# An RWKV-7 recurrence in chunks: one joined state product, products by turns, and preparation, inverse and finish cut into smaller pieces

## The chip, the cores and the metric

The kernel runs on one core of a Trainium2 chip. A core has a tensor engine (PE, with its weight loads PEld), a vector engine (DVE), a scalar engine (ACT), GpSimd (POOL) and a queue of DMA issues on SyncE (SP). Each works through its own list of instructions in order and waits on semaphores of the others. The metric is the device time of one execution in microseconds.

## The reference

One decoder block over 1024 tokens of width 1024, in float32: an input projection, RWKV-7 time mixing (8 heads of 64), attention over keys that an indexer selects, gates, an output projection and an MLP. The change lies in the time mixing. Per token and head, with a 64 x 64 state S:

```
def step(S, inp):
    r_t, w_t, k_t, v_t, a_t, b_t = inp
    sa = jnp.einsum('bhvk,bhk->bhv', S, a_t)
    S = (S * w_t[:, :, None, :] + sa[..., None] * b_t[:, :, None, :]
         + v_t[..., None] * k_t[:, :, None, :])
    return S, jnp.einsum('bhvk,bhk->bhv', S, r_t)
...
y = ((y - mean) * lax.rsqrt(var + RWKV_GN_EPS) * gn_w + gn_b)
y = (y + bonus) * gate
```

The mean and variance are per head and token; `bonus` is a dot product of r, k and r_k times v.

## The kernel before

The recurrence is computed in 16 chunks of 64 tokens, in 4 groups of 4 chunks. What one group needs is made by two Python generators while the chunks of the group before it run:

- `prep(g, G)` (L871 on), for each of four pairs of heads p: `elem(p)` loads `zt` and `zv`, makes decay products with a scan (`L`) and exponentials (`Pt`), and from them the operands `X` and `B`. Then PE multiplies B by X for each of the two heads and the four chunks (tile `sm<-X,B`), and DVE writes the masked result into `LT` (L938), the transposed B beside it (L946) and `bv` (L953). It yields 17 times.
- `invert(g, G)` (L957 on) inverts the triangular 64 x 64 blocks of `LT`. The 16 x 16 diagonal blocks go to DRAM (`md`) and come back as `Z` with another layout; 28 small DVE operations (L998, L1000) invert them; the result goes to DRAM (`mz`, with a transposed copy `Zt` made on ACT, L1002) and comes back as `R16` and `P16`. Then products `sm<-R,bd`, `sm<-bd,Q`, again `sm<-R,bd` (32 wide) and `sm<-P,bd` fill in the larger blocks, with copies on ACT (L1027, L1032, L1045, L1049) and transposes on DVE (`R<-LT`, L1034) between. It yields 5 times.

`chunk(g, G, c)` (L1053 on) has three steps, each ended by a yield:

1. `A` takes LT times WV for the upper half, then X times the state `cur` (tile `sbd`); ACT copies `rhs` (L1068).
2. `W` is the inverted LT times `rhs`; ACT copies it into `WV` (L1073).
3. `Bp` is the state product over all 128 rows, output in PSUM partitions 0 to 63; eight DVE operations (L1082) write the new state as Bp times decay plus `St`, which POOL made of the old state at the chunk's start (L1059). Then the output products go into partitions 64 to 127 of `A`, and ACT copies `Y` (L1089).

After every second chunk `finish(tt, Yt)` (L1092 on) normalises 128 tokens: scaling by gn_b and gate on DVE (L1103), by gn_w on ACT (L1105), mean and variance, a reciprocal root of ten small DVE operations, four transposes (`sm<-cst,Y`), a product and a sum.

Between these pieces the loop pulls units of a filler: `fill` (gates and one branch projection, 192 units of three products `dn`, 512 columns each) until the last group, `fill2` (branch and output projection, 96 units) in it. Numbers at the top say how many: `FILL`, `FIL3` (filler units behind each of the 12 steps of a group) and `AHEAD` (pieces of the next group's preparation and inverse behind each step); a finish's second piece comes `FIN_LAG` steps later. A scheduler then orders every engine's list when the program is built, keeping the dependences, with the order of the source as priority; `pe()` ties each PE instruction behind the one 32 places before it.

## Time and profile before

| | us |
|---|---|
| median of 3 runs (lowest, highest) | 1817.76 (1809.3, 1817.8) |
| the profiled execution | 1819.81, its span 1818.0 |
| PE busy in the span | 1697.3 |
| DVE busy | 1320.5 |
| ACT busy | 895.2 |
| POOL busy | 833.7 |

In the rows below, L and a number is a line of the kernel; an instruction shows engine, line, operation, tiles written and read, its shape and the number of equal ones. In brackets stands the idle time of the engine ahead of it and what ended that. Records of PE overlap and their ends are modelled, so steps from start to start say more than durations.

### The profile page before, as it was taken

How to read it: one execution, taken by the hardware profiler on the slowest of the kernel's cores; microseconds unless marked ns; L12 is line 12 of the kernel's file. 1: busy time of each engine (PE TensorE's matmuls, PEld its weight loads, DVE VectorE, ACT ScalarE, POOL GpSimd, SP SyncE). 2: the span in 40 equal slices, each digit the busy share in tenths (PEclk: the TensorE clock that was granted, in tenths of full speed). 3: DMA queues.
4: the chain of work that ended last, by engine and by line, in shares of the span. 5: the costliest groups of instructions: out<-in, count | busy, mean ns of one | idle time of the engine just before them, and what ended most of it. 6: DMA issues, size and time to landing. Idle time of an engine off the chain costs nothing.

```text
span 1818.0 us, 27188 instructions
## 1 busy us (share of the span) xinstructions
PE 1697.3 (93%) x9554; PEld 1424.4 (78%) x9554; DVE 1320.5 (73%) x2601; ACT 895.2 (49%) x1751; POOL 833.7 (46%) x761
## 2 busy tenths in 40 slices
PE   6999899849999999989898898999999999999997
PEld 6988887738788777777777797977888888888885
DVE  5689955996777454578666746699988875874988
ACT  5375664717777534245435425463444444444453
POOL 1522566324353334243423532286666656545552
PEclk9999999969999998799878999999999999999999
DMA  5230343212311355336436559415544549653444
GB/s 170 79 116 30 115 141 110 64 41 85 123 35 36 134 138 151 84 109 172 121 88 183 158 159 327 127 53 186 172 147 141 177 145 329 186 162 99 141 148 140
DMA packets 268287, 242.04 MB, mean 133 GB/s; under 512 B 64284, under 2 KB 206934, under 8 KB 268150
## 3 DMA queue, kind: packets, MB, share of 16 engines
q1 hardware_dynamic: 268150, 240.30, 42.3%
q8 instruction: 75, 1.23, 0.3%
q14 instruction: 62, 0.51, 0.1%
HBM read 164.76 MB, written 75.50 MB: 132 GB/s over the span
## 4 chain that ended last, share of the span: by engine, by line
PE 61%; DVE 18%; DMA 6%; POOL 4%; ACT 4%; issue 4%; SPq 1%; POOLq 0%; DVEq 0%; ACTq 0%
PE up L189 24%; PE dn L189 15%; PE sm L189 9%; DVE jk L577 3%; PE sm L192 2%; PE ch L189 2%; PE acc L189 2%; PE dn L243 1%; PE dn L244 1%; DVE w L1328 1%; PE dn L242 1%; DVE Zt L998 1%; PE acc L243 1%; POOL h L1328 1%; PE acc L242 1%
## 5 line engine op out<-in xcount | busy, mean ns | idle before, releaser
L189 PE MATMUL dn<-hT,w 128*128 128x512 f32 (+1 forms) x1488 | 379.5, 402 | 8.3 <-ACT last L673 7.5
L189 PEld LDWEIGHTS dn<-hT,w 128*128 128x128 f32 (+1 forms) x1488 | 274.0, 189 | 67.5 <-ACT last L673 10.1
L189 PE MATMUL up<-h,w 128*128 128x512 f32 x1344 | 312.1, 393 | 6.4 <-DVE w L1328 3.1
L189 PEld LDWEIGHTS up<-h,w 128*128 128x128 f32 x1344 | 252.3, 189 | 63.3 <-DVE w L1328 5.0
L1328 DVE TENSOR_TENSOR w<-st,w 128x512 fp32r<-128x512 f32 x216 | 213.5, 1022 | 75.6 <-ACT w L1327 75.5
L210 POOL TENSOR_TENSOR w<-st,w 128x1024 fp32r<-128x1024 f32 (+2 forms) x75 | 179.7, 2397 | 164.6 <-ACT w L209 139.1
L189 PE MATMUL up<-w 128*128 128x512 f32 x1008 | 246.1, 390 | 2.7 <-DVE w L1328 2.7
L189 PEld LDWEIGHTS up<-w 128*128 128x128 f32 x1008 | 188.6, 188 | 44.5 <-DVE w L1328 5.4
L1327 ACT ACTIVATE w<-st 128x512 fp32r<-128x512 f32 x216 | 127.9, 624 | 158.3 <-PE up L189 49.7
L1621 POOL TENSOR_TENSOR st<-wb,wb 128x512 f32<-128x512 f32 x80 | 120.7, 1512 | 93.9 <-DVE w L1328 73.8
L1483 POOL TENSOR_TENSOR c<-st 128x512 f32<-128x512 f32 x80 | 124.6, 1565 | 52.0 <-DMA st<-in_w_ffn_up 26.2
L209 ACT ACTIVATE w<-st 128x1024 fp32r<-128x1024 f32 (+2 forms) x91 | 94.7, 1041 | 42.0 <-PE acc L244 15.0
L577 DVE TENSOR_SCALAR_CACHE_REDUCE jk<-room,cand 128x384 bf16<-128x384 int16 (+2 forms) x96 | 92.6, 1008 | 15.1 <-ACT jk L590 14.1
L1494 POOL TENSOR_TENSOR C<-C 128x512 f32<-128x512 f32 x64 | 75.5, 1180 | 59.1 <-ACT C L1493 59.1
L243 PE MATMUL dn<-w,hT 128*128 128x256 f32 (+1 forms) x320 | 92.1, 289 | 6.3 <-DVE w L210 6.3
L780 POOL TENSOR_SCALAR sm<-sm,rs 128x128 f32<-128x128 f32 (+7 forms) x64 | 47.8, 748 | 105.1 <-DVE rs L779 55.2
L590 ACT ACTIVATE jk<-room,neg 128x512 bf16<-128x512 int16 (+2 forms) x96 | 78.4, 819 | 33.4 <-POOL neg L598 21.8
L242 PE MATMUL dn<-w,hT 128*128 128x256 f32 (+1 forms) x320 | 92.0, 290 | 0.9 <-ACT hT L272 0.9
L244 PE MATMUL dn<-w,hT 128*128 128x256 f32 (+1 forms) x320 | 92.0, 290 | 0.0
L1328 DVE TENSOR_TENSOR w<-c,w 128x512 fp32r<-128x512 f32 x80 | 82.7, 1046 | 0.4
L189 PE MATMUL sm<-w 128*128 128x512 f32 x288 | 81.1, 389 | 0.0
L1327 ACT ACTIVATE w<-c 128x512 fp32r<-128x512 f32 x80 | 48.8, 627 | 64.4 <-PE up L189 52.0
(336 smaller groups left out, 3546.3 us busy)
## 6 DMA issues: line engine op xcount, KB each, us to landing
st<-hcd SPq DMA_DIRECT2D x112, 256.0 KB
st<-in_w_in SPq DMA_DIRECT2D x54, 512.0 KB
st<-in_w_ffn_up SPq DMA_DIRECT2D x36, 512.0 KB
hcd<-C SPq DMA_DIRECT2D x16, 1024.0 KB
wb<-in_w_ffn_down SPq DMA_DIRECT2D x64, 256.0 KB
hcd<-kc SPq DMA_DIRECT2D x16, 768.0 KB
zd<-ev SPq DMA_DIRECT2D x20, 512.0 KB
gzd<-ev SPq DMA_DIRECT2D x32, 256.0 KB
```

The lines of the kernel that those rows point to most:

```text
L189: pe(nc.tensor.matmul(*args, **kw))
L209: nc.scalar.activation(hi, st[0:rows, 0:n], AF.Copy)
L210: (eng or nc.gpsimd).tensor_tensor(lo, st[0:rows, 0:n], hi.bitcast(F32), op=OP.subtract)
L242: nc.tensor.matmul(ps, l[0], r[0], start=start, stop=False, skip_group_check=shared)
L243: nc.tensor.matmul(ps, l[0], r[1], start=False, stop=False, skip_group_check=shared)
L244: nc.tensor.matmul(ps, l[1], r[0], start=False, stop=stop, skip_group_check=shared)
L577: nc.vector.tensor_scalar(junk, src[b], cand[:, j:j + 1], None, op0=OP.is_ge, op1=OP.add, accum_out=cnt[:, j:j + 1])
L590: nc.scalar.activation(junk, src[b], AF.Sign, bias=neg[:, j:j + 1], accum_out=cnt[:, j:j + 1])
L1327: nc.scalar.activation(hi, src, AF.Copy)
L1328: return eng.tensor_tensor(lo, src, hi.bitcast(F32), op=OP.subtract)
L1483: nc.gpsimd.tensor_tensor(c, src, blocks[LEFT[p][2]], op=OP.add if LEFT[p][1] == "+" else OP.subtract)
L1621: nc.gpsimd.tensor_tensor(c, src, wblocks[RIGHT[p][2], f], op=OP.add if RIGHT[p][1] == "+" else OP.subtract)
```

## The change

- The state is joined into the product: `two` holds two 64 x 64 unit matrices one above the other; a product of `two` and the old state starts `Bp`, and the state products add to it. Two DVE operations then multiply by the decay. `St` and its POOL operation go.
- `in_turn` ties a product behind the one just before it. State and output products alternate, and so do the B,X products of the two heads of a pair.
- `hold` ties the first instruction of a piece of finish, inverse or preparation behind the latest instruction of a chunk's step on the same engine.
- `prep` issues the loads of the next pair a piece earlier and its element-wise work a piece later. `invert` has two more yields, `Zt` and the unit diagonal move to DVE. `finish` has three pieces before the last instead of one, and scales by gn_w on DVE from PSUM.
- The tables: `AHEAD` takes three pieces behind each of the first six steps instead of six behind three; the inverse's chain falls to step 7 and later; `FIL3` has fewer units in the first half. The start has its own table `FIRST`.

```diff
-FILL = [8, 2, 40, 3, 6, 22]
-AHEAD = [6, 6, 6, 0, 0, 0, 0, 0, 1, 1, 0, 10]
-FIN_LAG = 5
+FILL = [0, 0, 0, 0, 5, 7]
+AHEAD = [3, 3, 3, 3, 3, 3, 0, 2, 0, 1, 2, 1]
+FIN = [1, 1, 0, 1]
+FIRST = [3, 6] + [2] * 15 + [2, 9, 4, 14, 3, 3, 3, 2]
-FIL3 = [2, 3, 4, 4, 3, 4, 2, 4, 5, 3, 3, 5]
+FIL3 = [2, 2, 2, 2, 2, 3, 4, 4, 4, 4, 4, 4]
...
+    def in_turn(follows, *args, **kw):
+
+        ins = nc.tensor.matmul(*args, **kw)
+        if follows:
+            after(pe_hist[-1], ins)
+        pe(ins)
...
+            pair = [small(), small()]
+            for c in range(GC):
+                for e in range(2):
+                    r = slice(64 * e, 64 * e + 64)
+                    in_turn(c + e, pair[e][:, c * P:(c + 1) * P], B[r, c, :], X[r, c, p, :], start=True, stop=True)
             for e in range(2):
-                r = slice(64 * e, 64 * e + 64)
                 h = 2 * p + e
-                ps = small()
                 for c in range(GC):
-                    mm(ps[:, c * P:(c + 1) * P], B[r, c, :], X[r, c, p, :], start=True, stop=True)
...
+                if e and p < 3:
+                    ahead = elem(p + 1, *nx)
                 yield
...
+        yield
         for t in range(14, 0, -1):
             r = 15 - t
+            if t == 7:
+                yield
...
-        nc.scalar.activation(Zt[0:64], Z[0:64].rearrange("p s t -> p t s"), AF.Copy)
+        nc.vector.tensor_copy(Zt[0:64], Z[0:64].rearrange("p s t -> p t s"))
...
-                nc.vector.transpose(ce(R32[diag(h)]), LT[0:32, :, h:H:4, 0:32])
+                hold("V", nc.vector.transpose(ce(R32[diag(h)]), LT[0:32, :, h:H:4, 0:32]))
...
+    def hold(eng, ins):
+
+        if eng in own:
+            after(own[eng], ins)
+        return ins
...
-        St = rw.tile([P, 4, P], F32, name="St", tag="St")
-        nc.gpsimd.tensor_tensor(St, cur, G["pc"][:, c, :].unsqueeze(2).to_broadcast([P, 4, P]), op=OP.mult)
...
         Bp = chps()
+        mm(Bp[0:64], two, cur.rearrange("p q n -> p (q n)"), start=True, stop=False, skip_group_check=True)
         for h in range(H):
-            mm(Bp[0:64, h * N:(h + 1) * N], LT[:, h, 2 * C:3 * C], WV[:, h, :], start=True, stop=True)
+
+            in_turn(h, Bp[0:64, h * N:(h + 1) * N], LT[:, h, 2 * C:3 * C], WV[:, h, :], start=False, stop=True,
+                    skip_group_check=True)
+            in_turn(1, A[64:128, h * N:(h + 1) * N], LT[:, h, C:2 * C], WV[:, h, :], start=False, stop=True,
+                    skip_group_check=True)
...
-            for p in range(4):
-                nc.vector.scalar_tensor_tensor(nxt[r, p, r], Bv[0:64, p, e, :], G["pc"][r, c, p:p + 1],
-                                               St[r, p, r], op0=OP.mult, op1=OP.add)
+            own["V"] = nc.vector.tensor_tensor(nxt[r, :, r], Bv[0:64, :, e, :],
+                                    G["pc"][r, c, :].unsqueeze(2).to_broadcast([64, 4, N]), op=OP.mult)
...
-            nc.scalar.activation(o[1][:, cs], o[1][:, cs], AF.Copy, scale=pcol("gnw", p))
...
-        nc.vector.tensor_tensor(o[1], ps, o[1], op=OP.mult)
+        for p in range(4):
+            cs = slice(p * P, (p + 1) * P)
+            nc.vector.scalar_tensor_tensor(o[1][:, cs], ps[:, cs], pcol("gnw", p), o[1][:, cs],
+                                           op0=OP.mult, op1=OP.mult)
...
-                if fin:
-                    f_ = fin.pop(0)
-                    if f_ is not None:
-                        pull(f_, 1)
+                for f_ in fin:
+                    f_[1].pop(0) and pull(f_[0], 1)
+                fin[:] = [f_ for f_ in fin if f_[1]]
                 if g + 1 < NG:
                     n_, m = AHEAD[step], FIL3[step]
-                    for i in range(n_):
-                        pull(nxt, 1)
+                    for i in range(n_ + 1):
                         pull(filler, (i + 1) * m // (n_ + 1) - i * m // (n_ + 1))
-                    pull(filler, m - n_ * m // (n_ + 1))
+                        pull(nxt, i < n_)
```

Three places show how the lists move; a name's number is its buffer. On PE, in group 0, before the change, from the third chunk's last products (`ch<-WV,LT`, 16) to the first product of the inverse and the fourth chunk's start:

```order
L189 MATMUL ch<-WV,LT 64x64 x16
L189 MATMUL dn<-hT_6_85,w 128x512
L189 MATMUL dn<-hT_7_86,w 128x512 x3
L189 MATMUL dn<-hT_0_79,w 128x512 x3
L189 MATMUL dn<-hT_1_80,w 128x512 x3
L189 MATMUL dn<-hT_2_81,w 128x512 x3
L189 MATMUL dn<-hT_3_82,w 128x512 x3
L189 MATMUL sm<-R_7658,bd 128x16 x8
L189 LDWEIGHTS zb
L189 MATMUL ch<-zb 64x2
L189 MATMUL ch<-WV,LT 64x64 x8
L189 MATMUL ch<-sbd_6469,X 128x128 x4
```

With the change, from the fourth chunk's second step; `ch<-sbd,two` and the 16 `ch<-WV,LT` behind it are its third step:

```order
L190 MATMUL ch<-rhs,LT 64x64 x8
L190 MATMUL ch<-sbd_6472,two 64x512
L194 MATMUL ch<-WV,LT 64x64 x6
L190 MATMUL sm<-R_7793,bd 128x16 x8
L190 MATMUL dn<-hT_5_84,w 128x512 x3
L190 MATMUL dn<-hT_6_85,w 128x512 x3
L190 MATMUL dn<-hT_7_86,w 128x512 x3
L190 MATMUL dn<-hT_0_79,w 128x512
L190 MATMUL sm<-bd_7894,Q_7892 16x128 x8
L194 MATMUL ch<-WV,LT 64x64 x10
L190 MATMUL sm<-R_7928,bd 128x32 x8
```

The inverse's first products stood between the third and the fourth chunk, behind 16 filler products and the third chunk's `ch<-WV,LT`; now they stand inside the fourth chunk's third step, and ten of its products come behind them.

On DVE, group 0, before the change, around the third chunk's state update (`sbd_6469`):

```order
L170 SCALAR_TENSOR_TENSOR rq<-rb,rq 128x8
L168 TENSOR_TENSOR rb<-var,rq 128x8
L169 TENSOR_TENSOR rb<-rb,rq 128x8
L170 SCALAR_TENSOR_TENSOR rq<-rb,rq 128x8
L1082 SCALAR_TENSOR_TENSOR sbd_6469<-ch,pc,St 64x64 x8
L983 TENSOR_TENSOR bd_7895<-P_7659,cst 128x1024
L1034 STREAM_TRANSPOSE R_7952<-LT 32x256 x4
L887 SCALAR_TENSOR_TENSOR L<-cst,zt 128x256
L1122 TENSOR_TENSOR fo<-sm,fo 128x512
```

With the change, the middle of the chain `Z` and the third chunk's update (`sbd_6472`), and then the chain's end and the fourth chunk's update (`sbd_6471`):

```order
L1022 TENSOR_TENSOR Z<-Z,Zt 128x10x5
L1020 TENSOR_TENSOR Zt<-Z 128x54
L1112 TENSOR_TENSOR sbd_6472<-ch,pc 64x4x64
L1022 TENSOR_TENSOR Z<-Z,Zt 128x9x6
L1112 TENSOR_TENSOR sbd_6472<-ch,pc 64x4x64
L1152 SCALAR_TENSOR_TENSOR fo<-sm,par,fo 128x128 x2
L1020 TENSOR_TENSOR Zt<-Z 128x56
L1152 SCALAR_TENSOR_TENSOR fo<-sm,par,fo 128x128 x2
L1022 TENSOR_TENSOR Z<-Z,Zt 128x8x7
```

```order
L1020 TENSOR_TENSOR Zt<-Z 128x14
L1022 TENSOR_TENSOR Z<-Z,Zt 128x14
L1024 COPY Zt<-Z 64x256
L1002 TENSOR_TENSOR bd_7894<-P_7794,cst 128x1024
L1056 STREAM_TRANSPOSE R_7928<-LT 32x256 x4
L1112 TENSOR_TENSOR sbd_6471<-ch,pc 64x4x64 x2
L1136 SCALAR_TENSOR_TENSOR fo<-fo,par 128x128 x4
```

The chain straddled the second chunk's update before and lies around the third's now; the transposes `R` stood behind the third chunk's update and now stand between the end of `Z` and the fourth's.

On ACT, group 1, before the change, from the third chunk's `rhs` to its `WV`:

```order
L1068 ACTIVATE rhs<-ch 64x512
L1143 ACTIVATE ev<-dn 128x512
L1105 ACTIVATE fo<-fo,par 128x128 x3
L1112 ACTIVATE ysq<-Y 128x512
L1105 ACTIVATE fo<-fo,par 128x128
L1143 ACTIVATE ev<-dn 128x512
L209 ACTIVATE w<-st 128x1024
L1002 ACTIVATE Zt<-Z 64x256
L1073 ACTIVATE WV<-ch 64x512
```

With the change, the same stretch:

```order
L1094 ACTIVATE rhs<-ch 64x512
L1139 ACTIVATE ysq<-Y 128x512
L460 ACTIVATE ev<-dn 128x512
L217 ACTIVATE w<-st 128x1024
L1174 ACTIVATE ev<-dn 128x512
L1099 ACTIVATE WV<-ch 64x512
```

The scaling `fo` and the copy `Zt` are gone from between the two copies.

## Rows read from the trace of the kernel before

**Rows 1.** The page, part 1: busy time of each engine.
```profile
PE 1697.3 (93%) x9554; PEld 1424.4 (78%) x9554; DVE 1320.5 (73%) x2601; ACT 895.2 (49%) x1751; POOL 833.7 (46%) x761
```
**Rows 2.** Groups: stretch, length, busy per engine (instructions), granted clock, DMA share, GB/s.
```profile
712.95:820.96 108.01, 100.56 (x674) 83.01 (x673) 66.03 (x192) 43.51 (x96) 34.88 (x40) 0.81 0.34 91
820.96:907.73 86.77, 79.74 (x614) 65.44 (x612) 61.38 (x187) 40.51 (x88) 36.50 (x32) 0.94 0.53 148
907.73:997.41 89.68, 80.77 (x568) 65.91 (x569) 57.16 (x182) 37.79 (x80) 29.98 (x28) 0.83 0.48 132
997.41:1069.75 72.34, 64.18 (x548) 56.50 (x547) 41.68 (x89) 28.08 (x42) 34.30 (x22) 0.98 0.51 158
```
**Rows 3.** The same view of two stretches.
```profile
717.50:751.70 34.20, 34.20 (x155) 26.82 (x155) 17.42 (x56) 8.83 (x25) 5.20 (x9) 0.50 0.20 62
...
799.50:871.10 71.60, 66.21 (x526) 54.11 (x524) 58.87 (x174) 38.82 (x85) 28.83 (x30) 1.00 0.60 173
```
**Rows 4.** Timeline of PE: start, duration of the merged records, instruction.
```profile
673.86 0.60 PE L189 MATMUL sm<-f,cst 128*128 128x256 f32 x2
674.10 30.32 PE L189 MATMUL dn<-hT,w 128*128 128x512 f32 x132
...
716.54 2.73 PE L189 MATMUL sm<-P,bd 128*128 128x32 f32 x16 [2.83 <-ACT bd L1045]
...
1048.97 1.90 PE L189 MATMUL ch<-WV,LT 128*64 128x64 f32 x32 [1.74 <-ACT WV L1073]
...
1055.39 1.14 PE L189 MATMUL ch<-WV,LT 64*64 64x64 f32 x16
1056.46 1.16 PE L189 MATMUL ch<-sbd,X 128*128 128x128 f32 x8
```
**Rows 5.** Halves of the groups, DVE alone: length, busy, clock, DMA share, GB/s.
```profile
712.95:778.71 65.76, 36.91 (x117) 0.74 0.29 78
778.71:820.96 42.25, 29.12 (x76) 0.92 0.41 112
820.96:862.71 41.75, 32.88 (x112) 1.00 0.62 173
862.71:907.73 45.02, 28.49 (x76) 0.89 0.44 125
907.73:966.27 58.54, 41.58 (x137) 0.83 0.38 103
966.27:997.41 31.14, 15.58 (x45) 0.84 0.66 186
```
**Rows 6.** Groups of lines, 615 to 1093: busy us, mean ns | idle before, releaser.
```profile
L1105 ACT ACTIVATE fo<-fo,par 128x128 f32<-128x128 f32 x32 | 11.3, 391 | 24.4 <-DVE fo L1103 24.4
...
L1034 DVE STREAM_TRANSPOSE R<-LT 32x256 f32<-32x256 f32 x16 | 7.0, 434 | 30.0 <-ACT LT L1027 29.9
...
L1002 ACT ACTIVATE Zt<-Z 64x256 f32<-64x256 f32 x4 | 2.5, 629 | 10.0 <-DVE Z L1000 10.0
...
L998 DVE TENSOR_TENSOR Zt<-Z 128x14 f32<-128x14 f32 x8 | 1.4, 176 | 25.1 <-DMA Z<-md 25.0
```
**Rows 7.** Timelines of ACT and PE, chunk 2 and the inverse's first product.
```profile
785.17 0.63 ACT L1002 ACTIVATE Zt<-Z 64x256 f32<-64x256 f32 x1 [4.04 <-DVE Z L1000]
785.71 0.57 ACT L1073 ACTIVATE WV<-ch 64x512 f32<-64x512 f32 x1
...
786.33 3.18 PE L189 MATMUL ch<-WV,LT 128*64 128x64 f32 x32 [3.21 <-ACT WV L1073]
...
793.20 1.85 PE L189 MATMUL sm<-R,bd 128*128 128x16 f32 x16
```
**Rows 8.** PE alone in two quarters of a microsecond: length, busy (records), clock.
```profile
1049.70:1049.95 0.25, 0.25 (x12) 1.00 0.00 0
1050.10:1050.35 0.25, 0.25 (x9) 1.00 0.65 205
```
**Rows 9.** Timeline of DVE: a product from PSUM, and a state update.
```profile
675.04 0.41 DVE L953 TENSOR_TENSOR bv<-sm,zv 128x256 f32<-128x256 f32 x1
...
788.42 1.73 DVE L1082 SCALAR_TENSOR_TENSOR sbd<-ch,pc,St 64x64 f32<-64x64 f32 x8 [1.58 <-PE ch L189]
```

More of the change, by code (lines that the diff above doesn't have):

```diff
@@ L858, in c3 @@
         return ap.rearrange("p (c t) -> p c t", c=GC)
+    two = rw.tile([P, C], F32, name="two")
+    for i in range(2):
+        nc.scalar.activation(two[64 * i:64 * i + 64], ident[64 * i:64 * i + 64, 64 * i:64 * i + 64], AF.Copy)
     zb = rw.tile([P, C], BF16, name="zb")
@@ L878, in prep, with loads @@
         nc.gpsimd.memset(scl[64:128], 1.0)
-        def elem(p):
+        def loads(p):
             z = rw.tile([P, 4, GT], F32, name="zt", tag="zt", bufs=1)
@@ L907, in elem @@
             return zv, sq, f, B
-        ahead = elem(0)
+        nx = loads(0)
         yield
+        ahead = elem(0, *nx)
         for p in range(4):
@@ L913, in prep @@
             if p < 3:
-                ahead = elem(p + 1)
+                nx = loads(p + 1)
             ps = small()
@@ L929, in prep @@
             yield
+            pair = [small(), small()]
[3 more added lines that the diff above has]
+                    in_turn(c + e, pair[e][:, c * P:(c + 1) * P], B[r, c, :], X[r, c, p, :], start=True, stop=True)
             for e in range(2):
-                r = slice(64 * e, 64 * e + 64)
                 h = 2 * p + e
-                ps = small()
                 for c in range(GC):
-                    mm(ps[:, c * P:(c + 1) * P], B[r, c, :], X[r, c, p, :], start=True, stop=True)
-                for c in range(GC):
-                    nc.vector.scalar_tensor_tensor(LT[:, c, h, 0:P], ps[:, c * P:(c + 1) * P], scl[:, c, h:h + 1],
-                                                   gmask, op0=OP.mult, op1=OP.mult)
+                    nc.vector.scalar_tensor_tensor(LT[:, c, h, 0:P], pair[e][:, c * P:(c + 1) * P],
+                                                   scl[:, c, h:h + 1], gmask, op0=OP.mult, op1=OP.mult)
+                if e and p < 3:
+                    ahead = elem(p + 1, *nx)
                 yield
@@ L1019, in invert @@
         bd2 = rw.tile([P, 2 * GC, P], F32, name="bd2", tag="zt", bufs=1)
-        spread(nc.vector, bd2, P16, ind8)
+        hold("V", spread(nc.vector, bd2, P16, ind8))
         spread(nc.gpsimd, bd, A32, ind4)
@@ L1050, in invert @@
         yield
-    Ycur = [None]
+    Ycur, own = [None], {}
+    def hold(eng, ins):
+        if eng in own:
+            after(own[eng], ins)
+        return ins
     def chunk(g, G, c):
@@ L1067, in chunk @@
         rhs = rw.tile([64, RW], F32, name="rhs", tag="rhs", bufs=1)
-        nc.scalar.activation(rhs, A[0:64], AF.Copy)
+        own["A"] = nc.scalar.activation(rhs, A[0:64], AF.Copy)
         yield
@@ L1080, in chunk @@
             r = slice(64 * e, 64 * e + 64)
-            for p in range(4):
-                nc.vector.scalar_tensor_tensor(nxt[r, p, r], Bv[0:64, p, e, :], G["pc"][r, c, p:p + 1],
-                                               St[r, p, r], op0=OP.mult, op1=OP.add)
-        for h in range(H):
-            mm(A[64:128, h * N:(h + 1) * N], LT[:, h, C:2 * C], WV[:, h, :], start=False, stop=True,
-               skip_group_check=True)
+            own["V"] = nc.vector.tensor_tensor(nxt[r, :, r], Bv[0:64, :, e, :],
+                                    G["pc"][r, c, :].unsqueeze(2).to_broadcast([64, 4, N]), op=OP.mult)
         if ci % 2 == 0:
             Ycur[0] = rw.tile([P, RW], F32, name="Y", tag="Y", bufs=2)
-        nc.scalar.activation(Ycur[0][64 * (ci % 2):64 * (ci % 2) + 64], A[64:128], AF.Copy)
+        own["A"] = nc.scalar.activation(Ycur[0][64 * (ci % 2):64 * (ci % 2) + 64], A[64:128], AF.Copy)
         yield
@@ L1260, in hybrid_block @@
     pull(first, 1)
-    pull(filler, FILL[0])
-    for _ in range(17):
+    for n_ in FIRST:
+        pull(filler, n_)
         pull(first, 1)
-        pull(filler, FILL[1])
-    pull(filler, FILL[2])
-    pull(first, 99)
     fin = []
@@ L1290, in hybrid_block @@
                 pull(f_, 1)
-                fin += [None] * FIN_LAG + [f_]
+                fin.append((f_, list(FIN)))
         pull(nxt, 99)
-    pull(filler2, FILL[5])
-    for f_ in fin:
-        if f_ is not None:
-            pull(f_, 1)
+    for f_, due in fin:
+        while due:
+            due.pop(0) and pull(f_, 1)
+            pull(filler2, FILL[5])
     pull(filler2, 9999)
```

40 lines of the change are left out of this document (22 added, 18 removed).

## The prediction

> **What bounds the kernel now.** I read the page first, then the stretches, the waits, the timelines of single engines. The page gives TensorE (PE) 93% of the span [rows 1], but its spans overlap, so that share says little. The stretches say more [rows 2]: cut at the first `rhs` copy of each group, the three groups that also prepare the next one last 108.0, 86.8 and 89.7 us (284.5 together); the last, which prepares nothing, 72.3. The work beside them is the same kind, so the difference is what a group pays for preparation and inverse. The granted clock falls there too: 0.81, 0.94 and 0.83 of full, and in one piece of 34 us PE stood at the lower level, 1.2 GHz, throughout, while the neighbouring 72 us had 2.4 GHz [rows 3]. Before that fall PE had sat idle for the inverse (2.8 us before the `P` products), then it ran mostly the small products of preparation [rows 4].
>
> PE's own need is much less. At full clock 16 records of 64 columns take 1.14 us with a tail of 0.2, so 0.93; X times state 0.9; a 512-column filler record 30.32 / 132 = 0.23 [rows 4]. (An f32 product has two records; 32 in a row take 1.90 with tail.) A chunk is 0.93 + 0.9 + 0.93 + 1.86 = 4.6 us, four are 18.4. Preparation takes 16 X,B records for each of four pairs (128 columns like X times state, so 0.11 each and 7.2 a group) and some 6 of other products; the inverse four times 1.8; the filler 3 records a unit, 0.68 us. A group needs some 65 us of the 87 to 108 it gets: PE is not the bound, it waits.
>
> For what? In the first two chunks of a group, for VectorE (DVE): 32.9 of 41.8 us busy in group 1, the one with full clock there [rows 5], the preparation's chain going to and fro between DVE, ScalarE (ACT) and PE. In the last two (chunks 2 and 3, counted from 0 in each group), for queues blocked at the head: DVE stood 30 us before the transposes `R`, 25 us before the first inverse step (a DRAM round trip), ACT 24 us before the finish's scaling and 10 us before the copy `Zt` [rows 6]. The last two cost PE directly: at 785.17 `Zt` had held ACT for 4.04 us, the chunk's `WV` copy stood behind it, and PE's products came 3.21 us late [rows 7].
>
> **The change, part by part.** The sum is made against the profiled execution, 1819.8 us (span 1818.0), 2.0 us above the median of the runs.
>
> *Turns.* The state products (columns 0 to 63 of the array) and output products (64 to 127) now alternate, as do X,B of the two heads (rows 0 to 63, 64 to 127). The trace has such neighbours only where one series ends and the next begins: there a quarter of a microsecond holds 12 live records, a little later, inside the series, 9 [rows 8]. So pairs overlap. I take the same for the rows. Taken as full overlap: a chunk's 32 records fall from 1.86 to 0.95, X,B from 7.2 to 3.6 us a group. None and all are the bounds: 0 and 0.9 x 16 + 3.6 x 4 = 29 us.
> The trace thus has overlap for different columns of one row set. The Trainium skill, "TensorE: Matmul & The Clock Gate", Part 3, says LDWEIGHTS overlaps with matmuls in flight only when the row group differs. By that rule the column pairs gain nothing and the sum would be up to 15 us higher; the rows at the border speak against it.
>
> *Joined state.* The POOL product `St` goes; the old state is added by a product with `two`, 512 columns of f32. Nearest row: 256 columns, two records in 0.60 us with tail, so about 0.43 more for each doubled record: 0.86 us [rows 4], between 0.4 and 1.3. It stands in PE's order right before the state products, so it takes back what the turns give the chunk. On DVE eight updates of 1.73 us become two over 64x256; nearest is the 128x256 product from PSUM, 0.41 [rows 9], so 0.8: 0.9 us less a chunk, on the chain from state to state.
>
> *Finish.* ACT loses the four `gnw` scalings; DVE's one product over 512 becomes four with a scalar, plus about 0.7 us each time. `Zt` moves to DVE too. ACT's head of queue is free for `rhs`, `WV` and `Y`: waits like the 3.2 us at 786 go.
>
> *Preparation over six steps.* Three pieces a step with two filler units, instead of six. DVE's need in chunks 0 and 1 falls only from 32.9 to about 32 (two updates less 1.9, finish plus 0.7), so it stays the bound; the loads `zt` are issued a piece earlier. Floor 32, ceiling today's 41.8 (58.5 and 65.8 in the other groups, whose first halves had 0.83 and 0.74 of the clock). I take 40, nearest the group that had full clock throughout.
>
> *The inverse, a chunk later.* This speaks against the change. Its chain `Z` used to straddle chunk 1's update, now chunk 2's; `R,bd` used to stand behind 16 filler records and now stands inside chunk 3's own products, with the R transposes ahead of chunk 3's update on DVE. Costs: the last LT write lies about 8 us behind chunk 1's update (my estimate: the fourth pair's X,B comes after the state product); the round trip to `Z` is 6.3 us of DVE's waiting on average (25.0 in four) [rows 6]; then half the chain before chunk 2's update. So update to update about 20 us, PE needing 16. After it: the other half of Z with finish pieces 6 us, then 7.8 us from Zt's start to R,bd (785.17 to 793.20) [rows 7]: R,bd is ready 14 us behind, and PE, with 8 filler records and the chunk's first products, is there after 6 to 8. It waits some 6 us, and the whole chunk behind it. Then R,bd 1.85, filler of about 2, Q as long as R, the LT evictions, four transposes of 0.43 [rows 6, 7], update 0.8, some 9 in all: chunk 3 takes 23. Behind those transposes on DVE stand the state update and the next finish; PE's next X product waits for the update. Chunks 2 and 3: 43 us, against 42.3, 45.0 and 31.1 now [rows 5]. Bounds: PE's own need of 33, and 55 if the wait also brings the lower clock.
>
> *First stretch.* PE's order has 68 filler records instead of 132 between the last preparation product and R,bd: 15 us of cover for a chain that needs 20 or more: the two round trips of 6.3 and 7.8, and 28 DVE operations of 0.18 us and up [rows 6]. PE waits 5 to 10 us; 3.6 come back from X,B, and the filler set free lies behind the inverse, where PE idled 2.8 [rows 4]. Net 0, bounds -8 and +8.
>
> *Last group.* Fewer units a step, more in the tail, the same sum; the shorter update four times: -4.
>
> **Sum.** A group 40 + 43 = 83, three are 249 against 284.5: -35.5. Last group -4, first stretch 0. 1819.8 - 39.5 = **1780 us**. Most of it comes from group 0, which loses its low-clock piece.
>
> **Rivals.**
> 1. The inverse stalls nobody (the round trip lands earlier, or DVE reaches Z sooner): chunks 2 and 3 take PE's 33 us, a group 73, three 219: -65.5 - 4, 1750 us. For it: the last group runs densely. Against: the measured 7.8 us. And if preparation too runs at DVE's floor of 32, a group takes 65 and the time is 1726.
> 2. Turns don't overlap for columns: +15 us if PE decides everywhere, 1795. Against it stand the border rows.
> 3. No change: chunks 2 and 3 take 53 us because the wait for R,bd is followed by the lower clock, as after 713 us; three groups of 93 are 279, 1810 to 1820 us.
> 4. Slower: chunks 0 and 1 of each group at 1.2 GHz. Their PE need is then 2 x 28 = 56 us (9.2 chunk, 9.8 preparation, 13 units of 0.68) instead of DVE's 40; with 45 to 50 for the rest, since PE's 33 there doubles in part, a group takes 101 to 106 and the time is 1833 to 1848. It decides once a group takes over 97 us, which is more than 14 us of lower clock added to my 83. For it: two of three first halves fell now, and the first six steps have less filler than before. Against: X,B is half as long and spread, and group 1's first half kept full clock at 0.94 overall.
>
> **How the numbers follow.** Chances: forecast with its bounds (1767 to 1806) 0.38, rival 1 0.27 and its better form 0.06, rival 2 0.05, rival 3 0.14, rival 4 0.10. A measurement of this kernel can tell 0.5% (9 us) from no change. Faster by more than that: 0.38 + 0.27 + 0.06 + 0.05 = 0.76; within 0.14; slower 0.10. The range leaves out rival 4 and the best form of 1, and takes in rival 3's lower half: 1738 to 1816.
>
> **What would show it.** Distances between group starts (first `rhs` of each): 83 expected, 73 for rival 1, 93 for rival 3, over 97 for rival 4. PE's idle time before `R,bd` 128x16, three times 4 to 8 us, and DVE's before the transposes; neither there means rival 1. State updates two by two at 0.4 us. 32 records of a chunk's last step in 1.2 us with tail, not 1.9; if 1.9, rival 2. Granted clock of 0.9 or more in each group; under 0.75 is rival 4. ACT's waits before `fo` and `Zt` gone. I am wrong in kind if the group distances stay and these waits are gone all the same: then something I hold for hidden (DVE's preparation, or weights arriving) sets the pace.

## The result, and the profile after

The change makes the kernel slower: 1834.29 us median of 4 runs (1829.87 to 1836.5) against 1814.39 for the kernel before, now also the median of 4, ratio 1.0119 with a 95% interval of 1.0093 to 1.0145. The forecast was 1780 us. The profiled execution took 1829.87 us, the lowest of its four, so the traces differ by only 10 us where the medians differ by 20.

First the stretches of the changed kernel, cut at the same marks as [rows 2], with the first stretch ahead and what follows the recurrence behind (length, busy per engine, granted clock, DMA share, GB/s):

```profile
615.00:723.13 108.13, 93.08 (x521) 75.92 (x521) 50.27 (x125) 36.69 (x77) 40.38 (x37) 0.94 0.51 141
723.13:815.31 92.18, 80.03 (x605) 63.22 (x605) 51.94 (x155) 32.30 (x70) 27.59 (x28) 0.86 0.35 92
815.31:909.54 94.23, 82.28 (x614) 62.86 (x613) 58.73 (x179) 39.13 (x82) 29.68 (x29) 0.87 0.49 140
909.54:1006.53 96.99, 85.39 (x634) 67.08 (x634) 57.71 (x174) 39.41 (x81) 29.36 (x27) 0.88 0.47 131
1006.53:1074.52 67.99, 60.25 (x518) 49.85 (x517) 44.10 (x85) 27.84 (x42) 29.26 (x18) 0.95 0.54 170
1074.52:1827.90 753.38, 722.79 (x3466) 603.25 (x3464) 589.07 (x788) 331.18 (x576) 407.97 (x284) 0.99 0.51 168
```

Against before: first stretch +10.2, the three groups -1.1 together (283.4 against 284.5, where 249 was forecast), last group -4.3, the rest +5.1 (it was 748.25), sum +9.9, the difference of the spans (1827.9 against 1818.0).

But the mark moved. The first `rhs` needs no inverse; the `WV` behind it does. On ACT, where the first group starts, before and after:

```profile
712.95 0.59 ACT L1068 ACTIVATE rhs<-ch 64x512 f32<-64x512 f32 x1
...
732.86 0.59 ACT L1073 ACTIVATE WV<-ch 64x512 f32<-64x512 f32 x1 [8.47 <-PE ch L189]
```
```profile
723.13 0.59 ACT L1094 ACTIVATE rhs<-ch 64x512 f32<-64x512 f32 x1
...
727.41 0.59 ACT L1099 ACTIVATE WV<-ch 64x512 f32<-64x512 f32 x1
```

The 108.0 us of [rows 2] hold 20 us between these two copies. Cut at each group's first `WV` (826.6, 911.4 and 1002.4 before; 819.9, 913.6 and 1012.2 after), the start is 5.4 us shorter, the groups take 284.8 against 269.6, 15.2 more, and the last 62.3 against 67.3, 5.0 less. So the loss lies in the groups. The halves of the groups, DVE alone, beside [rows 5]:

```profile
723.13:762.72 39.59, 27.72 (x80) 0.87 0.32 101
762.72:815.31 52.59, 24.22 (x75) 0.85 0.37 84
815.31:856.98 41.67, 32.45 (x100) 0.87 0.44 140
856.98:909.54 52.56, 26.29 (x79) 0.87 0.53 139
909.54:949.33 39.79, 31.71 (x96) 0.87 0.36 117
949.33:1006.53 57.20, 26.01 (x79) 0.88 0.54 140
```

The first halves are the forecast's 40. The second take 53 to 57, not 43. Two rows of PE and two of other engines, from the groups of lines (615 to 1098 us; busy us and mean ns, then the idle time before and what ended it), say who waits:

```profile
L194 PE MATMUL sm<-X,B 64*128 64x128 f32 x256 | 21.5, 313 | 13.2 <-DVE B L915 11.1 <-DVE rq L171 2.1
L190 PE MATMUL sm<-R,bd 128*128 128x16 f32 x64 | 11.5, 326 | 17.5 <-DMA R<-mz 17.5
...
L936 DVE TENSOR_SCALAR scl<-sm 64x8 f32<-64x8 f32 x16 | 2.4, 152 | 25.1 <-PE sm L190 25.1
...
L908 ACT ACTIVATE f<-zt,par,par 128x256 f32<-128x256 f32 x16 | 9.6, 599 | 55.2 <-DMA zt<-zd 55.2
```

PE now waits for B and for the inverse's `R`; before, the X,B row had 3.4 us and this `R,bd` row none. DVE stands 25 us before `scl`, the first result of a pair's preparation; before, 6.8. ACT's head of queue is free of `fo` and `Zt` [rows 6], but stands 55 us before `f`; in the kernel before it was 19.

So two of the signs that the prediction named came together: the distances between the group starts stayed, and ACT's waits before `fo` and `Zt` went. That is its own sign of being wrong in kind: something that it held for hidden sets the pace. The granted clock of the groups is 0.86 to 0.88, neither the 0.9 it wanted nor rival 4's 0.75; DVE's wait before the transposes `R` is 34.3 us, 30.0 before.

### The profile page after: what moved, and what is told of

It is laid out like the page before. It is cut to its first block, busy times and chain, and to the rows that moved or that the text cites. A ratio compares the mean times of both kernels' runs of the same rounds, so it can differ in the third digit from the quotient of the medians.

```text
span 1827.9 us, 27113 instructions
## 1 busy us (share of the span) xinstructions
PE 1679.8 (92%) x9586; PEld 1396.9 (76%) x9586; DVE 1311.7 (72%) x2537; ACT 882.7 (48%) x1717; POOL 813.0 (44%) x741
## 4 chain that ended last, share of the span: by engine, by line
PE 58%; DVE 20%; DMA 9%; POOL 4%; ACT 4%; issue 4%; SPq 1%; DVEq 0%; ACTq 0%; POOLq 0%
PE up L190 23%; PE dn L190 13%; PE sm L190 8%; DVE jk L585 2%; DMA zt<-zd 2%; PE sm L200 2%; DVE w L1354 2%; PE acc L190 2%; PE dn L251 2%; PE dn L252 2%; PE dn L250 2%; DVE Z L1022 1%; PE ch L190 1%; DMA st<-in_w_out 1%; DMA st<-ytd 1%
## 5 line engine op out<-in xcount | busy, mean ns | idle before, releaser
L190 PE MATMUL dn<-hT,w 128*128 128x512 f32 (+1 forms) x1488 | 385.7, 406 | 8.2 <-ACT last L681 7.5
L190 PEld LDWEIGHTS up<-h,w 128*128 128x128 f32 x1344 | 251.1, 188 | 62.3 <-DVE w L1354 4.9
L598 ACT ACTIVATE jk<-room,neg 128x512 bf16<-128x512 int16 (+2 forms) x96 | 78.4, 819 | 33.4 <-POOL neg L606 21.8
```

Source lines behind the costliest of these rows:

```text
L190: pe(nc.tensor.matmul(*args, **kw))
L598: nc.scalar.activation(junk, src[b], AF.Sign, bias=neg[:, j:j + 1], accum_out=cnt[:, j:j + 1])
```

## The experiments

Ratios are to the kernel before, with their 95% intervals. Where halves or waits are given, they come from one profile of each kernel. "Free" in the expectations means without the ties of `hold`.

**The start's cover, the late element-wise work, the turns, the table.** The first four each change one of these in the changed kernel.

E1:
```diff
-FIRST = [3, 6] + [2] * 15 + [2, 9, 4, 14, 3, 3, 3, 2]
+FIRST = [3, 6] + [2] * 15 + [2, 9, 18, 0, 3, 3, 3, 2]
```


> Edit: in the changed kernel, the 14 filler units that stand between the first group's R,bd and bd,Q products stand before R,bd. Theory A (the inverse's wait is a matter of cover): PE's wait of 11.0 us before the first R,bd falls by 14 x 3 x 0.227 = 9.5 us to about 1.5, the first group starts at about 714 instead of 723, and the time falls by 8 to 10 us. Rival B (those units hid the evictions between the inverse's later products): the wait goes, but waits of 2 to 3 us each come up before bd,Q, the second R,bd and P,bd, and the time falls by 0 to 4 us.

Measured 1.0107 (1.0081 to 1.0133): no gain that can be told. In its profile the first `WV` comes 2.2 us earlier, but PE still waits 7.1 us at the first `R,bd`, where either theory wanted that wait nearly gone: the reply itself came later, `R,bd` at 700.9 instead of 697.6. So this edit did not take the wait away, and E9 tries a longer cover.

E2:
```diff
-        nx = loads(0)
+        ahead = elem(0, *loads(0))
...
-                nx = loads(p + 1)
+                ahead = elem(p + 1, *loads(p + 1))
```


> Edit: in the changed kernel, the loads and the element-wise work of the next pair are issued together at the place where the kernel before issued them (a piece earlier than in the change). Theory C (the late element-wise work makes PE wait for B): PE's waits for B of L915 ahead of the X,B products, 12 us in sum from 615 to 1098 us, go, as do the 4 us before the sq products, and the time falls by 8 to 14 us. Theory A (the inverse sets the second halves, DVE's own pace the first): first halves stay at 40 us, the time moves by 3 us at most either way.

Measured 1.0175 (1.0146 to 1.0205). Theory C falls: the earlier place is slower, PE's waits for B stay at 9.9 us. The loss of some 10 us is also more than the 3 that theory A allowed.

E3, in both places (`mm` for `in_turn`, and the old order of the lines):
```diff
-            in_turn(h, Bp[0:64, h * N:(h + 1) * N], LT[:, h, 2 * C:3 * C], WV[:, h, :], start=False, stop=True,
+            mm(Bp[0:64, h * N:(h + 1) * N], LT[:, h, 2 * C:3 * C], WV[:, h, :], start=False, stop=True,
...
-            pair = [small(), small()]
+                pair[e] = small()
```


> Edit: in the changed kernel, state products first and then output products, X,B head by head, none tied to the one before; all else is as changed. By the forecast's term the turns save 0.9 us a chunk and 3.6 a group: if PE decides everywhere the time rises by 29 us. Theory A (PE idles 26 us and more in a group): most of it falls into waits, the time rises by 5 to 15 us. Rival D (the tied order itself makes the chunk's state late): the time falls.

Measured 1.0077 (1.0046 to 1.0107): not slower, as both the forecast's term and theory A wanted, but faster than with turns by its ratio, though the two intervals just meet.

E4:
```diff
-AHEAD = [3, 3, 3, 3, 3, 3, 0, 2, 0, 1, 2, 1]
+AHEAD = [4, 4, 4, 4, 2, 2, 0, 1, 1, 1, 1, 1]
```


> Edit: in the changed kernel, the table takes 4, 4, 4, 4, 2, 2, 0, 1, 1, 1, 1, 1 pieces behind the twelve steps instead of 3, 3, 3, 3, 3, 3, 0, 2, 0, 1, 2, 1: preparation ends in the fifth step, the chain Z stands behind the sixth, R,bd behind the eighth, the rest one piece a step. Theory A (the inverse inside the last chunk costs some 10 us a group): second halves fall from 54 to about 46 us, first halves rise by 2 at most, the time falls by 12 to 24 us. Rival E (the preparation's pace is the cost that comes back): first halves rise from 40 to 46 to 50 us, the time stays within 6 us.

Measured 1.0147 (1.0119 to 1.0175), within 6 us of the change. The first halves take 42.6, 48.2 and 46.8 us, the second 44.3, 53.3 and 49.6: an earlier inverse moves time from the second halves to the first. The inverse's place alone is not the cause.

**One kind of turns, the old tables, the turns alone, the ties.**

E5 keeps the chunk's turns of the change and drops those of X,B, as E3 did.

> Edit: in the changed kernel, only the X,B products are head by head and untied again; the chunk's state and output products stay tied by turns. The run without any turns had a ratio of 1.0077 to the kernel before where the change has 1.0119, though PE's own work from 615 us to the recurrence's end is some 29 us more there. Theory D1 (the tied pair of X,B, eight products in a block that waits for B, is what costs): PE's waits for B of L915 fall from 12 to about 5 us as in that run, the ratio falls to 1.008 or below. Theory D2 (the chunk's tied products cost, because other products are set between them): the ratio stays at 1.011 to 1.014.

Measured 1.0114 (1.0079 to 1.0149): theory D2's range, but the interval reaches down to D1's, so this does not decide.

E6:
```diff
-AHEAD = [3, 3, 3, 3, 3, 3, 0, 2, 0, 1, 2, 1]
+AHEAD = [6, 6, 8, 0, 0, 0, 0, 0, 1, 1, 0, 10]
...
-FIL3 = [2, 2, 2, 2, 2, 3, 4, 4, 4, 4, 4, 4]
+FIL3 = [2, 3, 4, 4, 3, 4, 2, 4, 5, 3, 3, 5]
```


> Edit: the changed kernel with the tables of the kernel before for the groups: preparation 6, 6, 8 pieces behind the first three steps (the two more are the inverse's new yields), inverse 1, 1, 10 behind steps 8, 9 and 11, filler units 2, 3, 4, 4, 3, 4, 2, 4, 5, 3, 3, 5; the start's table stays. In PE's order R,bd then stands behind chunk 2's products, and no other product stands between chunk 3's. Theory A (the inverse inside chunk 3 costs some 10 us a group): second halves fall from 54 to 43 to 46 us, first halves rise by less than that, 40 to 45; the time falls by 12 to 25 us and the ratio to the kernel before is 0.998 to 1.005. Rival E (DVE's preparation in three steps costs in the first half what the second gains): first halves 48 to 54 us, ratio 1.009 to 1.014.

Measured 1.0114 (1.0079 to 1.015), rival E. The halves only trade: the first take 54.8, 63.4 and 55.6 us, the second 34.4, 38.2 and 35.7.

E7 adds to the kernel before `in_turn` and both of its uses, as the diff of the change has them.

> Edit: the kernel before, with both kinds of products tied by turns and nothing else of the change (state products first in each pair, output products second; St, tables, finish and inverse as before). By the forecast's term PE's work falls by 29 us and the time by as much if PE decides. Theory A (PE waits for others in every group): the work falls by 25 us or more, the waits take most of it, the time falls by 2 to 10 us. Theory D (the ties make the order worse): the time rises by 3 to 12 us.

Measured 0.998 (0.996 to 1.0001). PE is 26 us less busy than in [rows 1], the time the same within the interval's end:

```profile
PE 1670.9 (92%) x9554; PEld 1398.0 (77%) x9554; DVE 1321.2 (73%) x2601; ACT 894.7 (49%) x1751; POOL 837.7 (46%) x761
```

E8:
```diff
     def hold(eng, ins):
-        if eng in own:
-            after(own[eng], ins)
         return ins
```


> Edit: the changed kernel without the ties that set a piece's first instruction behind the chunk's latest on its engine (hold does nothing). Theory F (these ties make the element-wise work and Z late): PE's waits for B, sq and R,bd, 24 us in the groups, fall by a third or more, the time falls by 6 to 15 us. Theory A: the pieces' places are set by the tables, the time moves by 4 us at most; against the ties' purpose, the state's update may come later behind preparation on DVE and the time rise by 5 us or more (rival G).

Measured 0.9963 (0.9939 to 0.9986): the largest step of all, 1.56% or 28 us below the change, and a little faster than the kernel before. Theory F holds in kind, with a gain two to four times the 6 to 15 us it expected. Its rows of `X,B`, `scl` and `f` beside those of the change (groups of lines, 615 to 1098 us), and its halves:

```profile
L194 PE MATMUL sm<-X,B 64*128 64x128 f32 x256 | 22.4, 296 | 4.6 <-DVE B L915 4.6
...
L936 DVE TENSOR_SCALAR scl<-sm 64x8 f32<-64x8 f32 x16 | 2.4, 150 | 0.6 <-PE sm L190 0.5
...
L908 ACT ACTIVATE f<-zt,par,par 128x256 f32<-128x256 f32 x16 | 9.6, 598 | 38.5 <-DMA zt<-zd 38.5
```
```profile
727.64:761.28 33.64, 25.00 (x85) 1.00 0.46 122
761.28:804.74 43.46, 26.95 (x78) 0.88 0.38 99
804.74:841.27 36.53, 30.01 (x95) 1.00 0.47 147
841.27:893.56 52.29, 29.92 (x72) 0.80 0.54 139
893.56:927.76 34.20, 26.87 (x92) 0.98 0.45 140
927.76:983.24 55.48, 30.78 (x89) 0.92 0.55 142
```

DVE's wait before `scl` is gone, PE's for B down from 11.1 to 4.6 us, each first half 5 to 6 us shorter with a clock of 0.98 and more. Only part of the 55 us before `f` goes, 38.5 stay. Part of that gain is idle time and part is clock: PE's idle time in the three first halves falls from 4.7, 6.2 and 6.2 us to 0, 1.6 and 3.6, and its busy time from 34.9, 35.4 and 33.6 to 33.6, 34.9 and 30.6 at the higher clock. Whether the lower clock could have gone with the ties in place was not tried. How the ties work can be seen in the changed kernel where group 0 ends. DVE:

```profile
806.23 0.68 DVE L902 TENSOR_TENSOR_SCAN L<-cst,zt 128x256 f32<-128x256 f32 x1
...
817.11 0.16 DVE L936 TENSOR_SCALAR scl<-sm 64x8 f32<-64x8 f32 x1 [10.14 <-PE sm L190]
```

ACT:

```profile
812.95 1.54 ACT L1071 ACTIVATE LT<-sm 32x256 f32<-32x256 f32 x4 [5.57 <-PE sm L190]
815.31 0.59 ACT L1094 ACTIVATE rhs<-ch 64x512 f32<-64x512 f32 x1 [0.83 <-PE ch L190]
...
816.33 0.40 ACT L905 ACTIVATE Pt<-L 128x256 f32<-128x256 f32 x1
```

`L` is ready at 806.9, and ACT stands idle 5.6 us in what follows; but the piece is pulled behind chunk 0's first step, so hold ties `Pt` and `f` (which follows it) behind that chunk's `rhs` copy, at 815.3. The next group's first pair starts 9 us late here; DVE's waits before `scl` at the three such places are 7.7, 10.1 and 6.1 us. The same two copies on ACT without the ties (E8), where `L` is written from 795.19 to 795.88:

```profile
796.10 0.40 ACT L905 ACTIVATE Pt<-L 128x256 f32<-128x256 f32 x1
...
804.74 0.59 ACT L1092 ACTIVATE rhs<-ch 64x512 f32<-64x512 f32 x1
```

`Pt` follows `L` in 0.2 us and stands 8.6 us ahead of `rhs`.

**Without the ties.**

E9: E8, and at the start
```diff
+FIRST = [3, 6] + [2] * 15 + [2, 9, 27, 0, 0, 0, 0, 2]
```


> Edit: the changed kernel without the ties of hold (ratio 0.996 to the kernel before), and at the start all 27 filler units of the inverse's last pieces set before the first R,bd. There PE waits 10.6 us for the inverse's reply and then runs 54 filler records that could have covered it. Theory A (cover): the wait falls to 2 us or less, the first group starts 8 to 10 us earlier, ratio 0.990 to 0.993. Rival B (the records hid evictions behind R,bd; the run with 14 units moved gained 2 us): bare waits of 2 to 3 us before each later product of the inverse, ratio 0.994 to 0.997.

Measured 0.9969 (0.9947 to 0.9992), rival B's range, but not by its mechanism: the waits it expected before the inverse's later products did not come (0.6 us before `P,bd`). The first `rhs` is at 715.9 instead of 727.6, but the first `WV` at 724.5 instead of 730.8, and the recurrence ends only 4.8 us earlier (1047.9 against 1052.7): the mark moved more than the work.

E10: the edits of E8 and E3 together.

> Edit: the changed kernel without the ties of hold and without products by turns. With hold, taking the turns away made the kernel faster (ratio 1.0077 against 1.0119). Theory H (with hold, the turns' products fell into the waits that hold made; without it PE's own work counts again): the time rises by 5 to 15 us against the run without hold, ratio 0.999 to 1.005. Rival D (the tied order itself costs, hold or not): the time falls, ratio below 0.994. If PE's work is covered by waits for DVE, ACT and the inverse in either case: within 4 us, 0.994 to 0.998.

Measured 0.9938 (0.9914 to 0.9962). Theory H falls: the time does not rise without the turns. Against E8 the intervals overlap, and they leave open whether dropping the turns still gains a little. The halves are not the same, though. Without turns the first take 35.1, 39.6 and 41.0 us, in which PE has no idle time, and the second 39.1, 46.0 and 45.1; E8 has 33.6, 36.5 and 34.2, and 43.5, 52.3 and 55.5. By these two profiles the turns shorten the first halves and lengthen the second, and the two cancel.

E11:
```diff
-        if eng in own:
+        if eng == "V" and eng in own:
```


> Edit: the changed kernel with hold on DVE alone (ACT's pieces are free). Theory F1 (the ties on DVE cost: scan, chain Z, bd, transposes and finish wait for the latest state update): ratio stays at 1.009 to 1.013. Theory F2 (the ties on ACT cost: the exponentials Pt, f and the finish's squares wait behind the chunk's latest copy, and B and sq behind them): ratio falls to 0.995 to 1.000. In between: both share it.

Measured 1.0025 (1.0003 to 1.0047): 0.62% of the 1.56 come with DVE's ties alone. The rest needs ACT's, either alone or together with DVE's; ACT's alone were not run.

E12: E9 with the tables of E6.

> Edit: as the run without hold and with the start's 27 units before R,bd, and with the kernel before's tables for the groups (6, 6, 8 pieces behind the first three steps; R,bd behind chunk 2's products). Theory A (R,bd between chunk 3's products holds the chunk): second halves of groups 1 and 2 fall from 52 and 56 to 44 to 46 us, first halves rise from 34 to 36 by 4 to 8, ratio 2 to 5 thousandths below the same run with the change's tables. Rival E (preparation in three steps costs more than that): first halves 45 us and more, ratio 3 to 8 thousandths above it.

Measured 1.0042 (1.0027 to 1.0057), 0.7% above E9: rival E. The new tables are a gain of this change, once the ties are off. They hold preparation over six steps, the inverse's place and the filler's, and were swapped whole, so this does not say which of the three gains. The halves of group 0 show the trade: 63.7 us at a clock of 0.77, then 34.4 at 0.97.

E13 and E14 leave hold in `prep` alone and in `invert` alone; elsewhere the instruction stands bare, as here:
```diff
-            hold("V", nc.vector.transpose(ce(R32[diag(h)]), LT[0:32, :, h:H:4, 0:32]))
+            nc.vector.transpose(ce(R32[diag(h)]), LT[0:32, :, h:H:4, 0:32])
```


> Edit: the changed kernel with hold on the preparation's three instructions of each pair alone (scan on DVE, Pt and f on ACT); inverse and finish are free. All ties together cost 1.56 per cent (ratio 1.0119 with, 0.9963 without), those on DVE alone 0.62. Theory F-prep (held scans and exponentials make B late for X,B): ratio 1.005 to 1.012, PE's waits for B of L915 stay near 12 us. Theory F-rest (the inverse and the finish are what suffers): ratio 0.995 to 1.000.

> Edit: the changed kernel with hold on the inverse's instructions alone (chain Z, bd and the R transposes, all on DVE); preparation and finish are free. Theory F-inverse (the chain is held behind the state update, so R,bd and the R transposes are late): ratio 1.002 to 1.006, about the DVE share of 0.62 per cent, second halves of the groups 2 us and more longer than without hold. Theory F-prep: ratio 0.995 to 0.999.

Measured 1.0096 (1.0063 to 1.013) for preparation's ties, 0.9956 (0.994 to 0.9972) for the inverse's. The three tied instructions of each pair carry most of the loss; the inverse's cost nothing that can be told. The halves agree: E13's are those of the change (40.9, 40.5, 40.3 and 52.9, 53.4, 56.6 us), E14's those of E8 (33.7, 35.0, 35.7 and 43.1, 51.2, 55.5). The ties of finish were not run alone.

E15: E10 with the state of the kernel before (`St` on POOL, no product of `two`):
```diff
-        mm(Bp[0:64], two, cur.rearrange("p q n -> p (q n)"), start=True, stop=False, skip_group_check=True)
...
+                nc.vector.scalar_tensor_tensor(nxt[r, p, r], Bv[0:64, p, e, :], G["pc"][r, c, p:p + 1],
+                                               St[r, p, r], op0=OP.mult, op1=OP.add)
```


> Edit: the changed kernel without hold and without turns (ratio 0.9938), and with the kernel before's state: St on POOL, eight updates on DVE, no product of two. By the forecast the joined state saves 0.9 us of DVE and costs 0.86 of PE a chunk, on a chain of 16 chunks: 0 to 15 us slower with the old state, ratio 0.994 to 1.002. Rival J (the product of two costs PE more than the update gives): faster, ratio 0.988 to 0.992.

Measured 1.0014 (0.9997 to 1.0032), 0.76% above E10: the joined state saves some 14 us (by the intervals 6 to 21), about 0.9 a chunk.

E16: E10 with E9's start.

> Edit: without hold, without turns, and the start's 27 units before the first R,bd. With turns, that cover moved the first group's start from 727.6 to 715.9 us in the profile and the median by nothing (0.9969 against 0.9963), the groups taking 7 us more. Theory A (cover adds up with the rest): ratio 0.988 to 0.991. Rival K (the filler units that cover the start are then missing in the groups): ratio 0.992 to 0.996.

Measured 0.9942 (0.9921 to 0.9963), rival K's range and no better than E10, though its profile is the shortest of all, a span of 1793.5. That execution is the lowest of E16's nine; by the runs its gain on the kernel before is some 10 us, 0.58%. Both E10 and E16 beat both kernels. Its halves:

```profile
714.34:754.45 40.11, 27.57 (x90) 0.96 0.33 100
754.45:799.44 44.99, 26.20 (x78) 0.87 0.43 101
799.44:840.12 40.68, 32.96 (x100) 0.98 0.51 156
840.12:883.95 43.83, 29.98 (x73) 0.96 0.60 159
883.95:924.94 40.99, 33.65 (x104) 1.00 0.43 129
924.94:969.18 44.24, 27.47 (x75) 0.96 0.59 158
```

E17 is E8 with the chunk's products plain, E18 is E8 with those of X,B plain.

> Edit: without hold; X,B by turns as in the change, the chunk's state and output products plain. Without hold the ratio was 0.9963 with both kinds of turns and 0.9938 with neither. Theory L (turns save PE time that PE then waits; where other products are set between the chunk's tied ones, they make the state late): ratio 0.992 to 0.995 here, as with neither. If the X,B turns are the loss: 0.996 to 0.998.

> Edit: without hold; the chunk's products by turns as in the change, X,B plain. Theory L: ratio 0.996 to 0.998, as with both. If the X,B turns are the loss: 0.992 to 0.995. If the four ratios agree within 0.002, the turns are worth nothing either way.

Measured 0.9948 (0.9927 to 0.9969) and 0.9954 (0.9936 to 0.9973). With E8 and E10 the four ratios lie between 0.9938 and 0.9963, and every interval meets the others: without hold the turns are worth nothing that can be told in the whole time.

## Why the prediction was wrong

The profiled execution took 1829.87 us, 49.6 more than the sum. In the sum's own terms: the groups took 34.4 more than 249, the start 10.2 more than its "net 0", what follows the recurrence 5.1 more than nothing, the last group 0.3 less than forecast. Within the groups the first halves together are 1.1 above three times 40, the second 33.4 above three times 43.

**The ties of hold: no term at all.** The forecast walks through turns, state, finish, preparation, inverse and start, and costs hold at nothing without saying so. It is 28 us (E8), most of it in preparation (E13). That is the step that failed first: an added order on a queue is an added wait. In the profiles the groups fall from 283.4 to 255.6 without the ties, 27.8 us: 16.7 in the first halves, 11.1 in the second. The forecast even counts "ACT's head of queue is free", where the ties put `Pt` and `f`, and with `f` the wait for `zt`, behind the chunk's copies.

**Chunks 2 and 3, "43 us".** Measured 52.6, 52.6 and 57.2. From update to update chunk 3 took 23.6, 22.4 and 21.0 against 23: this term came true. Chunk 2 took 25.6, 26.7 and 29.1 against 20. DVE in group 0, from chunk 1's update over the last LT write and the first step of Z to chunk 2's update:

```profile
754.46 0.85 DVE L1112 TENSOR_TENSOR sbd<-ch,pc 64x256 f32<-64x256 f32 x2
...
766.88 0.88 DVE L965 TENSOR_TENSOR LT<-sm,scl 128x128 f32<-128x128 f32 x4
...
773.76 0.18 DVE L1020 TENSOR_TENSOR Zt<-Z 128x14 f32<-128x14 f32 x1 [3.78 <-DMA Z<-md]
...
780.48 0.42 DVE L1112 TENSOR_TENSOR sbd<-ch,pc 64x256 f32<-64x256 f32 x1
```

The forecast's three parts were 8 us to the last LT write, 6.3 for the round trip, and the rest, 5.7, for half the chain. Measured, here and in groups 1 and 2: 12.4, 10.2 and 12.4; 6.0, 6.3 and 6.3; 7.1, 10.3 and 10.4. The round trip was right. The late LT write goes with the ties: without them (E8) it comes 1.5, 3.8 and 8.0 us behind chunk 1's update, with preparation's alone (E13) 12.6, 8.8 and 11.4. Without them chunk 2 takes 20.9, 23.8 and 23.0. The chain cost more than its steps of 0.2 us, since DVE stands in two of them beside POOL (last section). The remaining excess lies where the sum had no term: the next group's first `rhs` comes 10.8, 7.8 and 12.3 us behind the last update, 3.4 to 7.1 more than chunk 2's `rhs` behind chunk 1's.

The wait for `R,bd`, which the forecast made the core of chunk 3, was 3.8, 1.1 and 1.8 us in the groups, not some 6; the other 10.9 of the 17.5 stand at the start. Its 7.8 us from the start of `Zt` to `R,bd` came from a place where `R,bd` stood behind filler, so it was an upper bound: measured 5.8, 7.8 and 5.2. PE in chunk 3 of group 0:

```profile
788.16 0.51 PE L194 MATMUL ch<-WV,LT 128*64 128x64 f32 x10
792.46 3.57 PE L190 MATMUL sm<-R,bd 128*128 128x16 f32 x16 [3.79 <-DMA R<-mz]
795.86 4.12 PE L190 MATMUL dn<-hT,w 128*128 128x512 f32 x10
...
801.77 0.80 PE L194 MATMUL ch<-WV,LT 128*64 128x64 f32 x20
```

`R,bd` splits the chunk's tied products, 10 records ahead and 20 behind, so the state waits for the inverse; after the wait PE runs at 1.2 GHz (a granted clock of 0.51 from 792.4 to 796.0; 3.57 us where [rows 7] has 1.85), and the filler between takes 4.12. Still chunk 3 took what was forecast.

**What stays without the ties.** E8's groups, 255.6 us together, come near the forecast's 249 by two misses that cancel: the first halves 15.6 below it, the second 22.2 above. When the turns go too (E10, E16) the second halves of groups 1 and 2 fall from 52.3 and 55.5 to between 43.8 and 46.0, and the first rise to about 40. In E8 PE stands 4.1 and 4.9 us before `R,bd` in groups 1 and 2, in E10 there is no such wait; so the tied order seems to hold the chunk up at the inverse. That rests on one profile of each and was not followed further. With hold and turns gone and the start covered (E16) the halves are 40.1 to 41.0 and 43.8 to 45.0: the forecast's 40 and 43 came true, in a kernel without the two parts that it took for free and for a gain.

**The sum's mark.** "Most of it comes from group 0, which loses its low-clock piece": of its 108.0 us, 20 stand between the first `rhs` and `WV`, which the change takes to 4.3. That piece did go, but mostly because `rhs` moved behind the inverse: the sum kept `rhs` in its place ("net 0") and it came 10.2 us later, so start and piece together gave 5.4 us (`WV` at 727.4 instead of 732.9). By the `WV` cut the groups before take 269.6, and 249 would have been worth 20.6 us, not 35.5.

**Turns.** The overlap was as forecast: 30 of the 32 records in 1.09 us with tail, where [rows 4] has 1.90.

```profile
773.81 0.64 PE L190 MATMUL ch<-sbd,two 128*64 128x512 f32 x1
773.82 0.33 PE L194 MATMUL ch<-WV,LT 128*64 128x64 f32 x2
...
774.72 1.09 PE L194 MATMUL ch<-WV,LT 128*64 128x64 f32 x30
```

The Trainium skill, "TensorE: Matmul & The Clock Gate", Part 3, allows LDWEIGHTS this overlap only when the row group differs. The rows differ from it: these pairs share their rows and differ in columns. X,B gained less, 1.16 us for 16 records against 1.71 before. Rival 2 (no overlap) falls, and still the time gained nothing: E7 took 26 us off PE and at most some 7 off the time. The forecast had said that PE is not the bound, and its 40 and 43 have no term for the turns; it does not price what a fixed order costs the waits either.

**Joined state.** `two` took 0.91 us (773.81 to 774.72, forecast 0.86), the updates two by two at 0.41. Right in size; in the sum it appears only as the 4 us of the last group and the 0.8 of an update, and E15 shows some 14.

**Preparation over six steps: 40 us.** Right in the number, by a wrong reason: not DVE's pace, since without hold first halves took 34 to 37 (E8). Where they are 40 without hold (E10, E16), PE has no idle time in most of them. **Rival 4** (1.2 GHz in the first halves) did not come: the clock was 0.87 there. Its 1833 to 1848 holds the measured time by accident.

**First stretch, "net 0, bounds -8 and +8".** Measured +10.2 by the forecast's mark, -5.4 by `WV`. The wait at the first `R,bd` was 10.9, just above the 5 to 10 forecast:

```profile
697.60 3.56 PE L190 MATMUL sm<-R,bd 128*128 128x16 f32 x16 [10.87 <-DMA R<-mz]
```

But the 132 records of [rows 4] had covered it for longer than it took: there `R`'s load was issued at 696.5, and `R,bd` stood behind the records until 704.26; here the load was issued at 694.1 and `R,bd` ran 3.5 us later. The inverse's last copy is only 2.2 us later now.

**Last group, -4.** It came, 68.0 against 72.3, with +5.1 behind it: 47 more PE records stand behind the recurrence (3466 against 3419). The sum of -4 counted the tail as nothing more.

Rival 3 came nearest by the groups: 92 to 97, as it said, at 53 to 57 in the second halves. Its time of 1810 to 1820 lacks the 10.2 us of the start. Its cause, the lower clock behind the wait for `R,bd`, is not what the runs show: without hold alone (E8) the clock of a second half was 0.80 and the time 28 us less.

## What to carry to other kernels

Price every tie that a change adds to an in-order queue as a wait: find the instruction that it now stands behind and read when that one runs; here three tied instructions a pair cost some 24 us (1.0096 with them alone, 0.9963 without any). A saving on an engine that waits for others goes into its waits: 26 us off PE were worth 7 at most. And cut stretches at a mark that the change does not move, or the sum counts a shifted mark as a gain.
